# A safety margin in a planner's clock: operands of TensorE and freed buffers of the second layer count as ready later

## The chip, the core and the metric

The kernel runs on one core of a Trainium2 chip. The metric is device time in microseconds of one execution; lower is better. TensorE is PE in the profile, its weight loads are PEld, VectorE is DVE, ScalarE is ACT, GpSimd is POOL, SyncE is SP. SP only issues DMAs here; POOL issues some and computes a little.

## The reference, cut to what matters

Two layers over 512 rows of width 1024, all in float32. Layer 0 is a retention layer, layer 1 is a forgetting attention with 16 heads of width 64:

```python
q, k, v, g, f = jnp.split(h @ w_in, [FOX_W, 2 * FOX_W, 3 * FOX_W, 4 * FOX_W], axis=-1)
q = _rms_norm(q.reshape(b, s, 16, 64), q_gain) * (64 ** -0.5);  k = _rms_norm(k..., k_gain)
cum = jnp.cumsum(log_sigmoid(f + b_f), axis=1)
for qs in range(0, s, 128):              # 128 queries at a time
    logits = q[qs:qe] @ k[:qe].T + cum[qs:qe, None] - cum[None, :qe]
    p = softmax(where(causal, logits, -inf))
    outs.append(p @ v[:qe])
return (o * silu(g)) @ w_out
x = x + gate * y                         # after each layer; a last RMSNorm closes
```

## The kernel before, in words

**Arithmetic.** Each float32 operand of a matmul is split into a rounded upper half and the rest, and a product is three matmuls (`mm3`: upper x upper, upper x rest, rest x upper). For a weight tile `raw` (512 KB, loaded by SP) ACT casts the upper half `wh` and DVE subtracts to get the rest `wl`. One matmul of 128x128 by 128x512 is the unit of PE's work.

**Layer 1 in stages.** First come the projections of queries and keys (names `p<-wh,sf`, `p<-wh,big`: `big` holds the layer's normalised input, `sf` sums of it) and the forget gates (`wf`, `z`, `tri`, `cum_dram`). Then for each head: PE transposes the normalised rows `qn` and DVE and ACT write them as stacked halves `st` (`stacks`); PE multiplies queries by keys (`r<-st,st`, `scores`, four blocks a head); DVE adds the mask and the cumulated gates and writes `lg`; ACT takes the exponential; DVE the reciprocal; POOL multiplies `lg` by it; PE transposes `lg` (`r<-ident,lg`, `turn`); ACT and DVE write the halves `ph`; PE multiplies them by `v` (`r<-ph,v`, `values`, eight matmuls a head); DVE and ACT write `oT`. Between these steps PE works at projections (of the second half of q, k, v and of the gate g), which wait for nothing in the heads. At the end the output projection (`a<-wh,goh`) and the last norm follow.

**Buffers.** PE's results go to eight PSUM banks: kinds `p` (projections, at most six) and `r` (everything of the heads, at most four). A bank is used again when its last reader is done. All other tiles share pools of fixed slots in the same way.

**What sets the order.** The program is not written in the order in which it runs. Each call makes a `Task` with a priority; `Sched.order` then runs the whole program through a model of the engines, with a clock of its own: a task may start on its engine when all it depends on is done, `LAT` = 0.2 us after the end of a producer on another engine, and when the buffers it writes first are free. Each engine takes the task with the lowest priority number of those that may start. The order in which the model starts the tasks is the order in which they are emitted, engine by engine, all from one line (L472 in the profile's rows). On the chip each engine works through its list in that order, and waits on semaphores where the chip is later than the model. So a number in the model changes no instruction, only what stands ahead of what on each engine.

The two places of the model that the change touches are these:

```python
b.users -= 1
if b.users == 0 and b.kind is not None:
    free[self.kinds[b.kind][0]].append(b.slot)
    used[b.kind] -= 1
...
lat = self.LAT if t.eng != s.eng else 0.0 if t.eng == "PE" else 0.13
s.ready = max(s.ready, t.done + lat)
```

Of the kernel before, what the change touches and what calls it, by code (L numbers as in the profile page):

```python
# [26 lines left out]
PE = mybir.EngineType.PE  # L27
# [33 lines left out]
LATER = 4.0  # L61

GATE1 = "q k v g0"

LOOK = 30.0

# [130 lines left out]
class Sched:  # L197
# [117 lines left out]
    def order(self):  # L315

        import heapq
        tasks = self.tasks
        free = {k: list(range(n)) for k, (n, _) in self.phys.items()}
        used = {k: 0 for k in self.kinds}  # L320
        turn = {k: 0 for k in self.kinds}
        avail = {e: [] for e in self.ENG.values()}
        busy = {e: True for e in avail}
        ev, count, out, table = [(START, 0, -i, e, None) for i, e in enumerate(busy)], 0, [], None
        hw = dma = reach = 0.0
        soft, soft_wait, soon = [], [], []
        ticks = {-1: 0}
        left = sum(t.eng == "PE" for t in tasks)
        for t in tasks:
            t.wait, t.ready = len(t.deps), 0.0  # L330
            if not t.wait:
                heapq.heappush(avail[t.eng], (t.prio, t.seq, t))

        def fits(t):
            if t.eng == "SP" and t.prio > reach:
                return False
            need = {}
            t.new = [b for b in t.bufs if b.slot is None and b.kind is not None]
            for b in t.new:
                ph, cap = self.kinds[b.kind]  # L340
                need[ph] = need.get(ph, 0) + 1
                if turn[b.kind] != b.seq or used[b.kind] >= cap or len(free[ph]) < need[ph]:
                    return False
            return True

        now = 0.0
        while True:
            moved = True
            while moved:
                moved = False  # L350
                for e in avail:
                    if busy[e]:
                        continue
                    held, got = [], None
                    while avail[e]:
                        x = heapq.heappop(avail[e])
                        if fits(x[2]):
                            got = x[2]
                            break
                        held.append(x)  # L360
                    for x in held:
                        heapq.heappush(avail[e], x)
                    if got is not None and e == "DVE" and now < LOOK and any(
                            x.prio < got.prio - 1.0 and x.ready < now + 0.2 and fits(x) for x in soon):
                        heapq.heappush(avail[e], (got.prio, got.seq, got))
                        continue
                    if got is None and e == "PE" and now > 1.5 and self.idle is not None and self.idle.buf.slot is not None:

                        got = self.filler()
                    if got is None:  # L370
                        continue
                    moved = True
                    if self.idle is not None and e == "PE" and not got.filler and self.idle.buf in got.bufs:
                        self.idle = None
                    for b in got.new:
                        ph = self.kinds[b.kind][0]
                        b.slot = free[ph].pop(0)
                        used[b.kind] += 1
                        turn[b.kind] += 1
                    out.append(got)  # L380
                    got.start = now
                    if e == "PE":
                        tick = int(now / TICK)
                        if ticks.get(tick - 1, 0) < TICK_COLS and got.cols > 192:
                            got.cost *= 2.0
                        tick = int((now + got.cost) / TICK)
                        ticks[tick] = ticks.get(tick, 0) + got.cols
                    if e == "PE":
                        left -= not got.filler or got is self.first
                        reach = max(reach, got.prio) if left else now + 1e9  # L390
                    busy[e] = True
                    count += 1
                    end = now + got.cost
                    if got.table not in (None, table):
                        end += 1.3
                        table = got.table
                    heapq.heappush(ev, (end, 0, count, e, None))
                    if got.bytes:
                        if e == "POOL":
                            soft.append(got)  # L400
                            a = end + 0.6
                        else:
                            hw = max(hw, now + 0.05) + 0.45
                            a = hw + 0.6
                        heapq.heappush(ev, (a, 3, count, None, got))
                    else:
                        got.done = end
                        heapq.heappush(ev, (end, 1, count, None, got))
            if not ev:
                break  # L410
            now = ev[0][0]
            while ev and ev[0][0] <= now:
                _, what, _, e, t = heapq.heappop(ev)
                if what == 0:
                    busy[e] = False
                elif what == 3 and t.eng == "POOL" and t is not soft[0]:

                    soft_wait.append(t)
                elif what == 3:
                    dma = max(now, dma) + t.bytes / 360e3  # L420
                    t.done = dma + 0.5
                    if t.eng == "POOL":
                        t.done = now + t.bytes / 360e3 + 1.4
                    count += 1
                    heapq.heappush(ev, (t.done, 1, count, None, t))
                elif what == 1:
                    if t.bytes and t.eng == "POOL":
                        soft.pop(0)
                        if soft and soft[0] in soft_wait:
                            count += 1  # L430
                            soft_wait.remove(soft[0])
                            heapq.heappush(ev, (now, 3, count, None, soft[0]))
                    for b in t.bufs:
                        b.users -= 1
                        if b.users == 0 and b.kind is not None:
                            free[self.kinds[b.kind][0]].append(b.slot)
                            used[b.kind] -= 1
                    for s in t.next:
                        lat = self.LAT if t.eng != s.eng else 0.0 if t.eng == "PE" else 0.13
                        s.ready = max(s.ready, t.done + lat)  # L440
                        s.wait -= 1
                        if not s.wait:
                            count += 1
                            heapq.heappush(ev, (s.ready, 2, count, None, s))
                            if s.eng == "DVE":
                                soon.append(s)
                else:
                    if t in soon:
                        soon.remove(t)
                    heapq.heappush(avail[t.eng], (t.prio, t.seq, t))  # L450
        if ev or any(avail.values()):
            todo = {e: [(t.emit[1], [(b.kind, b.seq) for b in t.new]) for _, _, t in sorted(avail[e])[:4]]
                    for e in avail}
            raise RuntimeError(f"stuck at {now:.1f} of {len(tasks) - len(out)} tasks: {todo}, {used}, {turn}")
        self.end = now
        return out
# [98 lines left out]
def trunk(tc, x, c, positions, mod_w, mod_b, norm_g, ret_w_in, ret_w_out, fox_w_in, fox_b_f,  # L555
# [6 lines left out]
    with ExitStack() as es:  # L562
# [255 lines left out]
        def add(key, its):  # L818
            where[key] = len(items)
            items.extend(its)  # L820
# [93 lines left out]
        def gate_after(key):  # L914
            for _ in range(GATE1.split().count(key)):
                add(("e", len(items)), extra.pop(0))
# [969 lines left out]
```

## Time and profile before

| what | value |
|---|---|
| median of 3 runs | 714.42 us (714.22 to 714.66) |
| the profiled execution: its time, its span | 714.6 us, 712.6 us |
| PE, PEld busy | 700.3 us (98%), 576.7 us (81%) |
| DVE, ACT, POOL busy | 617.5 us (87%), 420.2 us (59%), 128.0 us (18%) |
| granted clock of PE, mean | 0.998 |
| HBM read, written | 113.35 MB, 4.25 MB |

The span is the time from the first to the last instruction; 2.0 us of the execution lie around it. Times in the rows below are counted from the span's start. A row of the timeline gives start, duration, engine, line, operation, output<-inputs, array size, shape, and in brackets how long the engine sat idle before it and which engine's instruction ended that; "x7" is seven instructions in a row. A matmul's shown duration is longer than the distance to the next one's start, because matmuls are pipelined: two rows of PE overlap. Layer 1 fills the span from about 420 us.

### The profile page before, as it was taken

The numbers are of one execution on the slowest core, as the hardware profiler recorded it, in microseconds if no ns is written. First come the engines' busy times: TensorE is split into PE (matmuls) and PEld (weight loads), VectorE is DVE, ScalarE is ACT, GpSimd is POOL, SyncE is SP. The second block draws the span as 40 slices with busy tenths as digits, with TensorE's granted clock in tenths as the row PEclk, the third lists the DMA queues.
The fourth block names the chain that finished last, engine by engine and source line by source line (L and its number), as shares of the span: only waits on it lengthen the run. The fifth ranks groups of instructions, "written<-read, shape, count | busy, mean of one in ns | idle before, by whom it ended". The sixth has DMA issues, their size and how long they took to land.

```text
span 712.6 us, 10207 instructions
## 1 busy us (share of the span) xinstructions
PE 700.3 (98%) x3383; PEld 576.7 (81%) x3383; DVE 617.5 (87%) x1268; ACT 420.2 (59%) x779; POOL 128.0 (18%) x175
## 2 busy tenths in 40 slices
PE   8999999999999999999999999999999999999995
PEld 6888888888888888888888887787877888888884
DVE  4799999888978996998998899699898998789925
ACT  5558564654365435865534565674777677779613
POOL 1001101100010001001000102014463564442011
PEclk9999999999999999999999999999999999999999
DMA  8992964647666766717669315668776696757002
GB/s 285 349 327 86 183 211 82 140 164 265 128 152 206 236 121 158 269 60 147 186 203 296 147 41 118 126 210 196 202 165 169 178 214 152 184 132 232 36 14 104
DMA packets 80724, 122.47 MB, mean 172 GB/s; under 512 B 7080, under 2 KB 39968, under 8 KB 80672
## 3 DMA queue, kind: packets, MB, share of 16 engines
q1 hardware_dynamic: 66176, 98.71, 43.2%
q0 software_dynamic: 14496, 23.10, 19.0%
q8 instruction: 27, 0.44, 0.3%
q14 instruction: 25, 0.20, 0.1%
HBM read 113.35 MB, written 4.25 MB: 165 GB/s over the span
## 4 chain that ended last, share of the span: by engine, by line
PE 82%; DVE 12%; ACT 3%; issue 2%; DMA 0%; POOL 0%; DVEq 0%; ACTq 0%; POOLq 0%
PE p L472 48%; PE r L472 17%; PE a L472 11%; PE s L472 6%; DVE wl L472 2%; DVE t L472 2%; DVE st L472 1%; DVE qn L472 1%; DVE xn L472 1%; DVE lg L472 1%; DVE ph L472 1%; ACT st L472 1%; ACT lg L472 1%; ACT wh L472 1%; DVE x L472 1%
## 5 line engine op out<-in xcount | busy, mean ns | idle before, releaser
L472 DVE TENSOR_TENSOR wl<-raw,wh 128x1024 fp32r<-128x1024 f32 x132 | 160.5, 1219 | 27.8 <-PE p L472 16.2
L472 ACT CAST wh<-raw 128x1024 fp32r<-128x1024 f32 x132 | 137.3, 1051 | 76.7 <-PE p L472 37.7
L472 PE MATMUL p<-wh,big 128*128 128x512 f32 x304 | 102.8, 400 | 0.0
L472 PE MATMUL p<-wh,sf 128*128 128x512 f32 x320 | 101.6, 392 | 0.0
L472 PEld LDWEIGHTS p<-wh,sf 128*128 128x128 f32 x320 | 60.0, 188 | 12.8
L472 PEld LDWEIGHTS p<-wh,big 128*128 128x128 f32 x304 | 56.8, 189 | 10.7
L472 POOL DMA_DIRECT2D raw<-in_ret_w_in x16 | 19.4, 1212 | 255.9 <-DMA raw<-in_mod_w 78.2
L472 PE MATMUL p<-wh,act 128*128 128x512 f32 x192 | 62.7, 393 | 0.0
L472 PE MATMUL p<-wl,sf 128*128 128x512 f32 x160 | 62.7, 392 | 0.0
L472 PE MATMUL p<-wl,big 128*128 128x512 f32 x152 | 60.7, 400 | 0.0
L472 POOL TENSOR_SCALAR lg<-lg,t 128x512 f32<-128x512 f32 (+1 forms) x64 | 46.9, 838 | 67.5 <-DVE t L472 64.5
L472 DVE SCALAR_TENSOR_TENSOR macc<-raw,csilu,macc 128x512 f32<-128x512 f32 x76 | 57.1, 753 | 0.8
L472 PE MATMUL p<-act,wh 128*128 128x512 f32 x160 | 53.4, 393 | 0.0
L472 ACT ACTIVATE lg<-lg,t 128x512 f32<-128x512 f32 (+1 forms) x64 | 35.7, 559 | 13.8 <-DVE t L472 13.5
L472 PE MATMUL p<-big,wh 128*128 128x512 f32 x128 | 43.6, 403 | 0.0
L472 PE MATMUL r<-act,sh 128*128 128x512 f32 x120 | 42.7, 391 | 0.2 <-DVE sh L472 0.2
L472 PEld LDWEIGHTS p<-wh,act 128*128 128x128 f32 x192 | 36.0, 188 | 7.3
L472 PE MATMUL p<-wh,go 128*128 128x512 f32 x112 | 39.2, 402 | 0.0
L472 PE MATMUL p<-wl,act 128*128 128x512 f32 x96 | 37.8, 394 | 0.0
L472 PEld LDWEIGHTS p<-wl,sf 128*128 128x128 f32 x160 | 30.0, 188 | 6.1
L472 PE MATMUL r<-st,st 128*128 128x512 f32 (+3 forms) x128 | 34.1, 337 | 0.5 <-DVE st L472 0.3
L472 PEld LDWEIGHTS p<-act,wh 128*128 128x128 f32 x160 | 29.8, 188 | 5.6
(213 smaller groups left out, 1592.9 us busy)
## 6 DMA issues: line engine op xcount, KB each, us to landing
raw<-in_ret_w_in SPq DMA_DIRECT2D x48, 512.0 KB, 5.3
raw<-in_mod_w SPq DMA_DIRECT2D x64, 256.0 KB, 6.0
raw<-in_fox_w_in SPq DMA_DIRECT2D x32, 512.0 KB, 4.6
raw<-in_ret_w_in POOLq DMA_DIRECT2D x16, 512.0 KB, 6.4
raw<-in_mod_w SPq DMA_DIRECT2D x16, 512.0 KB, 4.4
raw<-in_ret_w_out SPq DMA_DIRECT2D x16, 512.0 KB, 4.9
ck<-cum_dram SPq DMA_DIRECT2D x16, 448.0 KB, 4.8
x<-in_x SPq DMA_DIRECT2D x16, 256.0 KB, 5.9
```

The source lines that it names most:

```text
L472: getattr(eng, op)(*[real(v) for v in args], **{k: real(v) for k, v in kw.items()})
```

## The change

Three numbers are added to the model, and used only where its clock is past 420: an operand that another engine makes for PE counts as ready 0.8 us later than before, and a freed buffer (a PSUM bank or a slot of any pool) counts as free 0.5 us later.

```diff
+MARGIN, FREE, MARGIN_FROM = 0.8, 0.5, 420.0
...
+                elif what == 4:
+                    free[self.kinds[t.kind][0]].append(t.slot)
+                    used[t.kind] -= 1
...
                         if b.users == 0 and b.kind is not None:
-                            free[self.kinds[b.kind][0]].append(b.slot)
-                            used[b.kind] -= 1
+                            count += 1
+                            heapq.heappush(ev, (now + (FREE if now > MARGIN_FROM else 0.0), 4, count, None, b))
                     for s in t.next:
                         lat = self.LAT if t.eng != s.eng else 0.0 if t.eng == "PE" else 0.13
+                        if s.eng == "PE" and t.eng != "PE" and now > MARGIN_FROM:
+                            lat += MARGIN
```

No instruction is added, removed or resized. The lists of all engines stay as they were up to the forget gates of layer 1; behind that point most rows of PE, DVE and ACT have moved by a few places. (Line 472 of the kernel before is line 480 after, and buffer numbers count in the order of emission, so the same tile may carry another number.)

First place, PE, the first scores of the first head (about 493 to 495 us in the trace before). `qn` rows are the transposes whose result DVE and ACT turn into `st`; the first row with `st` is the one that needs it. Before, from the last transposes on:

```order
L472 MATMUL r_4852<-ident,qn_4742 128x128
L472 MATMUL r_4861<-ident,qn_4742 128x128
L472 MATMUL p_4751<-wh_4706,big_3988 128x512
L472 MATMUL p_4751<-wl_4797,big_3988 128x512
L472 MATMUL p_4751<-wh_4706,big_4000 128x512
L472 MATMUL p_4751<-wh_4706,big_3988 128x512
L472 MATMUL p_4751<-wl_4797,big_3988 128x512
L472 MATMUL p_4751<-wh_4706,big_4000 128x512
L472 MATMUL p_4766<-wh_4706,big_3988 128x512
L472 MATMUL p_4766<-wl_4797,big_3988 128x512
L472 MATMUL r_4890<-st_4753,st_4875 128x512
L472 MATMUL r_4890<-st_4760,st_4875 128x512
```

After, from the third matmul behind the last transposes on:

```order
L480 MATMUL p_4766<-wh_4710,big_3988 128x512
L480 MATMUL p_4766<-wl_4806,big_3988 128x512
L480 MATMUL p_4766<-wh_4710,big_4000 128x512
L480 MATMUL p_4766<-wh_4710,big_3988 128x512
L480 MATMUL p_4766<-wl_4806,big_3988 128x512
L480 MATMUL p_4766<-wh_4710,big_4000 128x512
L480 MATMUL p_4783<-wh_4710,big_3988 128x512
L480 MATMUL p_4783<-wl_4806,big_3988 128x512
L480 MATMUL p_4783<-wh_4710,big_4000 128x512
L480 MATMUL p_4783<-wh_4710,big_3988 128x512
L480 MATMUL r_4903<-st_4754,st_4879 128x512
L480 MATMUL r_4903<-st_4760,st_4879 128x512
```

Before, eight projection matmuls stand between the last transposes and the first scores; now it is twelve.

Second place, PE, the first value matmul of a late head (about 632 to 635 us in the trace before). The `lg` row is the last of the four transposes whose result ACT and DVE turn into `ph`. Before:

```order
L472 MATMUL r_6653<-ident,lg_6472 128x128
L472 MATMUL p_6621<-big_3979,wl_6210 128x512
L472 MATMUL p_6537<-big_3988,wh_6350 128x512
L472 MATMUL p_6537<-big_4000,wh_6350 128x512
L472 MATMUL p_6537<-big_3988,wl_6365 128x512
L472 MATMUL p_6537<-big_3988,wh_6350 128x512
L472 MATMUL p_6537<-big_4000,wh_6350 128x512
L472 MATMUL r_6673<-ph_6666,v_5916 128x512
L472 MATMUL r_6675<-st_6535,st_6613 128x512
L472 MATMUL r_6680<-ident,lg_6566 128x128
L472 MATMUL p_6537<-big_3988,wl_6365 128x512
L472 MATMUL p_6537<-big_3988,wh_6350 128x512
```

After:

```order
L480 MATMUL p_6505<-big_3988,wl_6325 128x512
L480 MATMUL p_6505<-big_3988,wh_6307 128x512
L480 MATMUL p_6505<-big_4000,wh_6307 128x512
L480 MATMUL p_6505<-big_3988,wl_6325 128x512
L480 MATMUL p_6505<-big_3988,wh_6307 128x512
L480 MATMUL p_6505<-big_4000,wh_6307 128x512
L480 MATMUL r_6688<-ph_6669,v_5905 128x512
L480 MATMUL r_6690<-st_6545,st_6613 128x512
L480 MATMUL r_6690<-st_6560,st_6613 128x512
L480 MATMUL r_6688<-ph_6675,v_5905 128x512
L480 MATMUL r_6688<-ph_6609,v_5927 128x384
L480 MATMUL r_6688<-ph_6624,v_5927 128x384
```

The piece of after begins two matmuls behind the last `lg` transpose: eight matmuls now stand ahead of the first value matmul, before it was six. The second value matmul, which needs DVE's half of `ph`, stood seven rows behind the first; now it stands three rows behind.

Third place, PE, the end of the attention: the last value matmuls of the last head and what is left behind them up to the output projection. Before, with nine more projection matmuls below the piece that is shown:

```order
L472 MATMUL r_6940<-ph_6901,v_6065 128x128
L472 MATMUL r_6940<-ph_6916,v_6065 128x128
L472 MATMUL p_6777<-big_3988,wl_6618 128x512
L472 MATMUL p_6777<-big_3988,wh_6598 128x512
L472 MATMUL p_6777<-big_4000,wh_6598 128x512
L472 MATMUL p_6777<-big_3988,wl_6618 128x512
L472 MATMUL p_6777<-big_3988,wh_6598 128x512
L472 MATMUL p_6777<-big_4000,wh_6598 128x512
L472 MATMUL p_6777<-big_3988,wl_6618 128x512
L472 MATMUL p_6871<-big_3988,wh_6598 128x512
L472 MATMUL p_6871<-big_4000,wh_6598 128x512
L472 MATMUL p_6871<-big_3988,wl_6618 128x512
```

After, up to the first row of the output projection:

```order
L480 MATMUL r_6959<-ph_6906,v_6094 128x128
L480 MATMUL r_6959<-ph_6913,v_6094 128x128
L480 MATMUL p_6839<-big_3988,wl_6573 128x512
L480 MATMUL p_6839<-big_3988,wh_6552 128x512
L480 MATMUL p_6839<-big_4000,wh_6552 128x512
L480 MATMUL p_6839<-big_3988,wl_6573 128x512
L480 MATMUL p_6839<-big_3988,wh_6552 128x512
L480 MATMUL p_6839<-big_4000,wh_6552 128x512
L480 MATMUL p_6839<-big_3988,wl_6573 128x512
L480 MATMUL a_7003<-wh_6678,goh_6946 128x512
```

Seven projection matmuls are left behind the last head where there were nineteen.

## The prediction

> **What bounds the kernel now.** I read the page's busy line and its chain first, then PE by stretches, then PE's waits, then the timeline at these waits.
>
> ```profile
> PE 700.3 (98%) x3383; PEld 576.7 (81%) x3383; DVE 617.5 (87%) x1268; ACT 420.2 (59%) x779; POOL 128.0 (18%) x175
> PE 82%; DVE 12%; ACT 3%; issue 2%; DMA 0%; POOL 0%; DVEq 0%; ACTq 0%; POOLq 0%
> ```
>
> PE is busy nearly always, yet 12% of the chain runs through DVE. So there are places where PE stood because DVE was late. The stretches tell where (columns: PE, PEld, DVE, ACT, POOL busy with counts, granted clock, DMA share, GB/s):
>
> ```profile
> 240.00:280.00 40.00, 40.00 (x188) 33.45 (x187) 35.09 (x74) 15.03 (x26) 4.83 (x4) 1.00 0.63 156
> 420.00:460.00 40.00, 39.73 (x176) 30.00 (x175) 32.53 (x60) 26.45 (x42) 4.89 (x4) 1.00 0.50 106
> 460.00:500.00 40.00, 39.19 (x179) 31.14 (x178) 38.22 (x69) 23.14 (x31) 9.61 (x14) 1.00 0.70 185
> 500.00:540.00 40.00, 39.58 (x213) 32.58 (x213) 34.44 (x94) 29.00 (x74) 21.22 (x31) 1.00 0.77 191
> 540.00:580.00 40.00, 39.64 (x212) 32.48 (x211) 37.29 (x90) 28.77 (x68) 20.33 (x30) 1.00 0.76 190
> 580.00:620.00 40.00, 39.46 (x219) 33.14 (x218) 34.37 (x85) 30.84 (x74) 20.77 (x32) 1.00 0.66 162
> 620.00:660.00 40.00, 39.55 (x221) 33.14 (x220) 35.54 (x86) 33.28 (x78) 13.80 (x22) 1.00 0.64 188
> ```
>
> A stretch of layer 0 has no idle PE at all; layer 1's six stretches have 237.15 of 240 busy, 2.85 us idle. The clock is full throughout, so no part of this is a slower clock. PE's waits between 420 and 660 are short and all on the heads' steps, none on a weight:
>
> ```profile
> PE r L472 <- DVE st L472: 0.6, 2, 0.4
> PE r L472 <- ACT ph L472: 0.5, 2, 0.3
> PE r L472 <- DVE qn L472: 0.4, 1, 0.4
> PE r L472 <- DVE oT L472: 0.3, 1, 0.3
> PE r L472 <- DVE t L472: 0.3, 1, 0.3
> PE r L472 <- ACT z L472: 0.3, 1, 0.3
> ```
>
> The idle time understates the loss, because a row's duration covers part of the gap behind it. The loss is the distance of two starts, less the usual distance. The usual one is in the chain: 192 matmuls in 42.89 us and 19 in 4.39 are 0.22 and 0.23 us each.
>
> ```profile
> 657.34 4.39 PE p L472 x19
> 661.73 42.89 PE a L472 x192
> ```
>
> Against that, these pairs of neighbours on PE, in order of time:
>
> ```profile
> 455.77 0.39 PE L472 MATMUL p<-wl,sf 128*128 128x512 f32 x1
> 456.44 0.40 PE L472 MATMUL r<-tri,z 128*16 128x512 f32 x1 [0.27 <-ACT z L472]
> ...
> 489.62 0.39 PE L472 MATMUL p<-wh,big 128*128 128x512 f32 x1
> 490.38 1.15 PE L472 MATMUL r<-ident,qn 128*128 128x128 f32 x8 [0.38 <-DVE qn L472]
> ...
> 494.13 0.40 PE L472 MATMUL p<-wl,big 128*128 128x512 f32 x1
> 494.81 1.48 PE L472 MATMUL r<-st,st 128*128 128x512 f32 x4 [0.28 <-DVE st L472]
> ...
> 551.73 0.39 PE L472 MATMUL p<-wl,big 128*128 128x512 f32 x1
> 552.45 0.52 PE L472 MATMUL r<-ident,lg 128*128 128x128 f32 x3 [0.33 <-DVE t L472]
> ...
> 633.59 0.62 PE L472 MATMUL p<-big,wh 128*128 128x512 f32 x2
> 634.53 0.50 PE L472 MATMUL r<-ph,v 128*128 128x512 f32 x1 [0.32 <-ACT ph L472]
> ...
> 650.33 0.62 PE L472 MATMUL p<-big,wh 128*128 128x512 f32 x2
> 651.09 1.27 PE L472 MATMUL r<-ph,v 128*128 128x512 f32 x7
> ```
>
> From 489.62 to 490.38 is 0.76, less 0.23 is 0.53 us lost, where the row shows 0.38 idle. The last pair shows no idle time and loses 0.76 less two steps, 0.3. Taken so for every neighbouring pair, each against the usual distance of its shape, 37 places between these first and last rows lose more than 0.04 us each, 7.3 us together. That is all a better order can bring in this stage, since projections stand ready to fill it. Fifteen places of 0.12 us or more hold 5.25 us; the other 22 hold 2.0, most of them the next matmul or two behind a wait.
>
> The 15 are of two kinds. At seven (2.7 us) the operand itself came last, as `st` at 494.81 and `ph` at 634.53. At eight (2.55 us) the operand had long been there and the PSUM bank came last. So at 552.45: POOL makes the `lg` that is transposed, yet the wait is put down to DVE, whose last read of the bank ends at 551.88 + 0.42 = 552.30.
>
> ```profile
> 551.88 0.42 DVE L472 TENSOR_TENSOR ph<-r,ph 128x256 fp32r<-128x256 f32 x1
> ```
>
> **A rule on headroom.** By the Trainium skill ("Perfetto Trace Analysis", section "Identifying the Most-Contended Engine"), matmul busy time is no good measure of how near TensorE is to its limit, and the busy share of the weight loads is better. The rows agree as far as the first half goes: 2.85 us idle stands for 7.3 lost. Measured by its second half, the six stretches hold 192.48 us of weight loads; at the 33.45 per 40 us of the unbroken stretch these would fill 230.2 us, so 9.8 us would be lost; regaining the share of it that the sum below regains of 7.3 (4.75) would give 714.4 - 6.4 = 708.0. I keep 7.3, because the mix of shapes differs.
>
> **The change part by part.** It adds and removes no instruction. What it does is to put more projection matmuls between a cause on PE and the PE instruction that needs its effect.
>
> *Operands, 0.8 us.* Of the seven waits the largest is 0.53 us, less than the margin. The pieces of the order agree at two of them: four matmuls more ahead of the first scores (4 x 0.23 = 0.9 against 0.45 lost there) and two more ahead of the value matmul (0.46 against 0.94 - 0.46 = 0.48). The others, counted in the order in the same way: over 0.7 us more at 456.44, 490.38 and 615, nothing more at 651.09, and 0.7 us less at 644. What grows holds 2.3 us; I take 2.2 gained of 2.7. Bounds: 0, if DVE and ACT run as much later as PE asks later; 2.7, if all goes.
>
> *Freed buffers, 0.5 us.* The eight bank waits are 0.13 to 0.52 us, the largest as long as the margin itself. DVE is late by a different amount at each place, as these waits show, and some places will meet more than 0.5, so I leave a quarter: 1.95 of 2.55 gained. Bounds 0 and 2.55. A slot of SBUF freed later makes some loads count later; that is hidden by the lead of the weights, below.
>
> *Followers.* The 22 small ones go with the waits that they follow: 2.0 x 0.75 = 1.5. Bounds 0 and 2.0.
>
> *New waits.* Other pairs move closer: the second value matmul stood seven rows behind the first and now stands three. If DVE's half of `ph` was just in time, this costs up to 4 x 0.23 = 0.9 us in a head; if it was early, nothing. Counted over the heads, five places lose distance and most of these by under 0.5 us. I take 0.9 us for all, bounds 0 and 3.
>
> *The end.* The chain shows 19 projection matmuls (4.39 us) between the last head and the output projection, and 7 are left now, 1.6 us. This cover is spent between the heads. It costs nothing while the last head's `ph` comes less than 1.6 us late, and the longest wait of that kind is 0.5. Behind it PE runs 42.89 us without a wait, and the rest hangs on that as before.
>
> Sum: 2.2 + 1.95 + 1.5 - 0.9 = 4.75, say 4.8 us. The profiled execution took 714.6 us (span 712.6 and 2.0 around it), so 709.8 for it; it lies 0.2 above the median 714.42, so 709.6 for the median.
>
> **Rivals.**
>
> *All of it goes:* the margins exceed every wait but one, so 714.4 - 7.3 = 707.1. Against it: places where the distance shrank.
>
> *DVE is the next bound.* In 460:500 it is busy 38.22 of 40, in 540:580 37.29. If those two stretches keep their waits (0.53 + 0.45 + 0.31 and 0.49 + 0.22 + 0.13 = 2.1 us) and the followers, 0.5, the gain is 2.2 and the time 712.2. For it: an order of PE cannot make DVE finish earlier. Against it: 1.8 us of DVE's 40 are free even there.
>
> *POOL's multiplications come late.*
>
> ```profile
> L472 POOL TENSOR_SCALAR lg<-lg,t x64: 361/688/1895, 501.9 to 651.7; 128x512 f32<-128x512 f32 x16, 128x384 f32<-128x384 f32 x16, 128x256 f32<-128x256 f32 x16, 128x128 f32<-128x128 f32 x16
> ```
>
> One takes 0.69 us in the median and up to 1.9. In the new order other DVE work lies beside them; if one in four heads loses the 1.2 us between, of which 0.7 is covered by the margin, that is 4 x 0.5 = 2 us less gain, 711.6. No PE wait above is on POOL. The Trainium skill ("SBUF — State Buffer", section "SBUF: two separate sides") says that VectorE and GpSimd lock a shared port pair for a whole instruction, which would make such spreads.
>
> *The waits only change places:* 714.4. For it: the order moved nearly all rows at once. Against it: every move is away from a late operand.
>
> *Slower: weights of the projections land late.* Freed slots count later, so loads may be asked for later. One landed so late that ACT sat for 4.86 us; and where the lead is smallest, DVE's `wl` ends at 458.78 + 1.22 = 460.0 and PE needs it at 461.55.
>
> ```profile
> 489.88 1.05 ACT L472 CAST wh<-raw 128x1024 fp32r<-128x1024 f32 x1 [4.86 <-DMA raw<-in_fox_w_in]
> 458.78 3.80 DVE L472 TENSOR_TENSOR wl<-raw,wh 128x1024 fp32r<-128x1024 f32 x3
> 461.55 0.39 PE L472 MATMUL p<-wl,sf 128*128 128x512 f32 x1
> ```
>
> A load that is 4.86 us late costs 4.86 - 1.5 = 3.3 us there; two of them outweigh 4.8 and give 714.4 + 6.6 - 4.8 = 716.2. Against it: no PE wait is on a weight.
>
> **How the numbers follow.** Chances: the sum as above (gain 3.3 to 6.3) 0.54; all of it 0.12; DVE the bound 0.16; POOL late 0.05; waits only moved 0.08; late weights 0.05. The time is that of the first, 709.6, its own range 708.1 to 711.1. The range 707.3 to 712.9 leaves out the last two and the outermost part of "all". Faster or slower counts from 0.2% on, 1.4 us, about what a measurement of this kernel can tell: faster 0.87, same 0.08, slower 0.05.
>
> **What would show it.** In the profile after: idle PE in 420 to 660 falls from 2.85 us to under 1.2, the waits on `st`, `qn`, `oT` and `z` vanish from the list, and DVE's share of the chain falls from 12% to under 6%. The output projection starts 4 to 5.5 us earlier than at 661.7 and still takes 42.9. Remaining waits should be on `ph` and on banks. I am wrong if PE waits on `wl` or `wh`, if POOL's `lg` appears as what PE waits for, or if DVE's idle time between 460 and 500 is gone with PE's waits still there.

## The result, and the profile after

| | before | after |
|---|---|---|
| median (lowest to highest) | 714.32 us (713.92 to 714.66) | 710.34 us (709.66 to 710.90) |
| the profiled execution, its span | 714.6, 712.6 us | 710.33, 708.4 us |

The ratio is 0.9946, with a 95% interval of 0.9934 to 0.9958: 4.0 us less. 709.6 was forecast, with a range of 707.3 to 712.9. All views below are of the kernel after unless another is named. First the page's busy line and the shares of the chain:

```profile
PE 695.8 (98%) x3383; PEld 576.0 (81%) x3383; DVE 616.8 (87%) x1268; ACT 419.6 (59%) x779; POOL 127.4 (18%) x175
PE 90%; DVE 6%; ACT 1%; issue 1%; DMA 1%; POOL 0%; DVEq 0%; POOLq 0%; ACTq 0%
```

The counts are the same, and no engine has less work to do; DVE's share of the chain has halved from 12%. Then layer 1 by stretches (PE, PEld, DVE, ACT, POOL busy with counts, granted clock, DMA share, GB/s):

```profile
420.00:460.00 40.00, 40.00 (x178) 30.76 (x178) 34.48 (x63) 27.53 (x43) 4.89 (x4) 1.00 0.50 106
460.00:500.00 40.00, 39.81 (x186) 32.15 (x185) 36.36 (x70) 23.07 (x34) 9.63 (x14) 1.00 0.70 187
500.00:540.00 40.00, 39.97 (x217) 33.37 (x216) 35.81 (x94) 30.54 (x77) 21.47 (x33) 1.00 0.75 190
540.00:580.00 40.00, 39.11 (x209) 32.03 (x208) 37.53 (x92) 27.16 (x64) 19.81 (x28) 1.00 0.74 184
580.00:620.00 40.00, 39.95 (x227) 33.97 (x226) 33.43 (x85) 31.44 (x78) 20.23 (x33) 1.00 0.71 174
620.00:660.00 40.00, 40.00 (x222) 34.31 (x220) 37.12 (x85) 33.79 (x76) 14.05 (x22) 1.00 0.64 189
```

PE's waits from 420 to 660 (us in total, times, longest):

```profile
PE r L480 <- DVE ph L480: 0.6, 2, 0.3
PE r L480 <- DVE st L480: 0.5, 2, 0.3
```

PE's idle time fell from 2.85 us to 1.16, and three quarters of it now lies in one stretch, 540 to 580, where DVE is busiest (37.53 of 40). The waits on `qn`, `oT`, `z` and ACT's `ph` have left the list. At the three places of before that the rows of the prediction showed (490.38, 494.81, 634.53), PE now goes straight on; the pairs in order of time are:

```profile
488.80 0.39 PE L480 MATMUL p<-wh,big 128*128 128x512 f32 x1
489.06 0.66 PE L480 MATMUL r<-ident,qn 128*128 128x128 f32 x4
...
493.66 0.61 PE L480 MATMUL p<-wh,big 128*128 128x512 f32 x2
494.11 1.01 PE L480 MATMUL r<-st,st 128*128 128x512 f32 x4
...
631.57 0.62 PE L480 MATMUL p<-big,wh 128*128 128x512 f32 x2
632.03 0.40 PE L480 MATMUL r<-ph,v 128*128 128x512 f32 x1
```

From 488.80 to 489.06 is 0.26 (0.76 before), from 493.66 to 494.11 is 0.45 for two matmuls, and 631.57 to 632.03 is 0.46. The first is only just so: the `qn` that it needs was done at 489.00, 0.06 us before; at the other two the operand had been done for 0.5 us. What is left is of another kind and at other places:

```profile
563.79 0.48 PE L480 MATMUL p<-wl,big 128*128 128x512 f32 x1
564.52 0.72 PE L480 MATMUL r<-st,st 128*128 128x512 f32 x2 [0.25 <-DVE ph L480]
...
570.46 0.62 PE L480 MATMUL p<-wh,big 128*128 128x512 f32 x2
571.38 0.44 PE L480 MATMUL r<-st,st 128*128 128x128 f32 x2 [0.29 <-DVE st L480]
572.12 0.63 PE L480 MATMUL r<-ident,lg 128*128 128x128 f32 x4 [0.31 <-DVE ph L480]
```

Scores do not read `ph`, and transposes of `lg` do not either: at 564.52 and 572.12 what came last was the bank that DVE's `ph` had been reading. At 571.38 the name misleads in another way. Scores do read `st`, but by the kernel's list the last of the `st` that these scores read was written in the first of the following two rows of DVE's timeline, and the second row makes other `st` from the bank that the scores need:

```profile
546.66 1.51 DVE L480 SCALAR_TENSOR_TENSOR st<-r,gain,st 64x512 fp32r<-64x512 f32 x2
...
569.81 1.51 DVE L480 SCALAR_TENSOR_TENSOR st<-r,gain,st 64x512 fp32r<-64x512 f32 x2 [0.54 <-ACT st L480]
```

The operand was done at 548.17, the bank was free at 571.32. The other wait on `st` in the list above, at 496.02, is of the same kind: its operand had been done for 2.4 us. Taken by the distance of two starts as in the prediction, with each wait followed by its instruction, the 37 places with 7.29 us are 22 with 3.96 now. The chain's last rows of PE:

```profile
650.51 2.30 PE p L480 x10
657.06 42.89 PE a L480 x192
```

The last instruction of ACT in the timeline of before:

```profile
708.03 0.72 ACT L472 ACTIVATE x<-x,t 128x512 f32<-128x512 f32 x1 [1.56 <-DVE t L472]
```

And in that of after:

```profile
703.36 0.72 ACT L480 ACTIVATE x<-x,t 128x512 f32<-128x512 f32 x1 [1.56 <-DVE t L480]
```

The output projection starts 661.73 - 657.06 = 4.67 us earlier, takes the same 42.89, and ACT's last instruction is 4.67 earlier too. Behind that the span goes on for 712.6 - 708.03 = 4.57 us before and 708.4 - 703.36 = 5.04 after, so 0.47 is lost at the last stores, and 4.2 us of the span is left. Of the 4.67, 0.40 was there before the first row that moved, in work that both kernels do in the same order, as the timeline's row of the transposes of `xn` shows. Before:

```profile
413.36 1.09 PE L472 MATMUL r<-ident,xn 128*128 128x128 f32 x8
```

After:

```profile
412.96 1.09 PE L480 MATMUL r<-ident,xn 128*128 128x128 f32 x8
```

### The profile page after: what moved, and what is told of

The parts are those of the page before. It is cut to its first block, busy times and chain, and to the rows that moved or that the text cites. A ratio compares the mean times of both kernels' runs of the same rounds, so it can differ in the third digit from the quotient of the medians.

```text
span 708.4 us, 10215 instructions
## 1 busy us (share of the span) xinstructions
PE 695.8 (98%) x3383; PEld 576.0 (81%) x3383; DVE 616.8 (87%) x1268; ACT 419.6 (59%) x779; POOL 127.4 (18%) x175
## 4 chain that ended last, share of the span: by engine, by line
PE 90%; DVE 6%; ACT 1%; issue 1%; DMA 1%; POOL 0%; DVEq 0%; POOLq 0%; ACTq 0%
PE p L480 56%; PE r L480 18%; PE a L480 11%; PE s L480 5%; DVE st L480 1%; DVE xn L480 1%; DMA vrow<-in_mod_b 1%; DVE t L480 1%; ACT st L480 1%; DVE x L480 1%; DVE ph L480 0%; DVE macc L480 0%; DVE wl L480 0%; DVE lg L480 0%; DVE big L480 0%
## 5 line engine op out<-in xcount | busy, mean ns | idle before, releaser
L480 PE MATMUL p<-wh,big 128*128 128x512 f32 x304 | 99.8, 397 | 0.0
L480 POOL TENSOR_SCALAR lg<-lg,t 128x512 f32<-128x512 f32 (+1 forms) x64 | 41.0, 671 | 72.1 <-DVE t L480 66.9
L480 DVE TENSOR_TENSOR ph<-r,ph 128x128 fp32r<-128x128 f32 (+1 forms) x64 | 30.6, 482 | 3.8 <-ACT ph L480 3.2
```

The lines of the kernel that those rows point to most:

```text
L480: getattr(eng, op)(*[real(v) for v in args], **{k: real(v) for k, v in kw.items()})
```

## The experiments

Each wait of 0.12 us or more was followed to the instruction that waits, in every kernel. "Old" are waits of instructions that are among the 15 of before; "new" are the others; "small" are places of 0.04 to 0.12. A wait counts as operand or bank by what was done last in the trace: the tile that the instruction reads, or the last read of the bank that it writes, both known from the kernel's list. "Left" is the number of projection matmuls behind the last head. All in us, the losses from the profiled execution of 420 to 660.

| kernel (operands, buffers) | left | old | new | of old and new: operand / bank | small | median | ratio, 95% interval |
|---|---|---|---|---|---|---|---|
| before (0, 0) | 19 | 5.25 | 0 | 2.69 / 2.56 | 2.04 | 714.4 | 1 |
| after (0.8, 0.5) | 7 | 0.98 | 2.00 | 0.21 / 2.77 | 0.97 | 710.34 | 0.9946 [0.9934, 0.9958] |
| operands only (0.8, 0) | 5 | 0.98 | 3.57 | 0.43 / 4.13 | 1.43 | 712.43 | 0.9976 [0.9966, 0.9986] |
| buffers only (0, 0.5) | 28 | 2.25 | 2.34 | 2.88 / 1.71 | 1.88 | 713.64 | 0.9991 [0.9983, 1.0000] |
| buffers twice (0.8, 1.0) | 0 | 0.29 | 4.42 | 2.65 / 2.07 | 1.42 | 714.16 | 0.9992 [0.9980, 1.0003] |
| negative (-0.2, 0) | 24 | 4.79 | 2.72 | 5.21 / 2.30 | 3.17 | 718.00 | 1.0053 [1.0040, 1.0066] |
| (0.8, 1.0 to 580, then 0.5) | 11 | 0.29 | 2.23 | 0.43 / 2.09 | 1.23 | 709.61 | 0.9933 [0.9920, 0.9947] |
| cost of `st` (0, 0) | 17 | 1.70 | 3.57 | 2.32 / 2.94 | 1.97 | 714.03 | 0.9997 [0.9989, 1.0006] |
| (0.4, 0.5) | 16 | 1.16 | 1.32 | 0.93 / 1.56 | 1.18 | 709.74 | 0.9936 [0.9924, 0.9949] |
| twice, with the gap filled | 0 | 0.30 | 2.21 | 0.45 / 2.05 | 1.37 | 712.42 | 0.9971 [0.9961, 0.9982] |
| (0.75, 0.55) | 12 | 0.37 | 1.94 | 0 / 2.31 | 1.23 | 710.03 | 0.9938 [0.9926, 0.9950] |
| (0.8, 0.5) to 540 only | 26 | 2.03 | 2.92 | 1.39 / 3.56 | 1.37 | 712.25 | 0.9967 [0.9955, 0.9979] |
| (0.3, 1.0 to 580, then 0.5) | 12 | 0.87 | 1.72 | 2.01 / 0.58 | 1.32 | 710.34 | 0.9947 [0.9935, 0.9960] |
| (0.4, 0.5), cost of `st` | 11 | 0.26 | 2.09 | 0.22 / 2.13 | 1.26 | 710.22 | 0.9946 [0.9934, 0.9959] |

### The two margins apart

```diff
-MARGIN, FREE, MARGIN_FROM = 0.8, 0.5, 420.0
+MARGIN, FREE, MARGIN_FROM = 0.8, 0.0, 420.0
```

> MARGIN 0.8, FREE 0: the operands' margin alone. Theory A (the 0.8 us on operands did the gain, the 0.5 us on buffers nothing): 710.3 us, 709.5 to 711.2, as the whole change; operand waits of 0.12 us or more on PE between 420 and 660 sum to under 0.5 us, bank waits to 2 to 3.3. Rival B (both margins share the gain, as the prediction's sum had it, 2.2 and 1.95): 712.0 to 712.8. Rival C (any other order of these instructions would have scattered around the same time): anywhere from 710 to 716, without a pattern in the waits.

712.43 us. The old operand waits are all gone, and of the old bank waits only 0.98 of 2.56 is left, though no bank counted later; but 3.14 us of bank waits are new. The largest, 1.05 us, is at the scores of 495.43, which lost 0.11 before (their own `st` was done at 493.02); and a wait on POOL's `lg` appears, the only one of any kernel here. Both in this kernel's timeline of PE:

```profile
495.43 0.50 PE L480 MATMUL r<-st,st 128*128 128x256 f32 x2 [0.88 <-DVE st L480]
...
652.84 0.66 PE L480 MATMUL r<-ident,lg 128*128 128x128 f32 x4 [0.27 <-POOL lg L480]
```

```diff
-MARGIN, FREE, MARGIN_FROM = 0.8, 0.5, 420.0
+MARGIN, FREE, MARGIN_FROM = 0.0, 0.5, 420.0
```

> MARGIN 0, FREE 0.5: the buffers' margin alone. Theory A: 713.6 to 715.0, within 0.1% of before; operand waits stay at 2 to 3.5 us and bank waits at 2 to 3. Rival B: 712.0 to 712.8, bank waits under 1 us. Rival C: no pattern.

713.64 us: the operand waits stay (2.88), the bank waits fall to 1.71. So the operands' margin alone brings 2.0 us and the buffers' 0.75 (its interval reaches to 1.0000), together 2.7; both at once bring 4.0. That the operands do it all is wrong, and so is that the two add: B's time came with the operands alone and not with the buffers alone. The second margin is worth 712.43 - 710.34 = 2.1 us once the first is there: it takes away a part of the bank waits that the first one makes, 4.13 to 2.77, and 0.46 of the small places.

### More, and less than nothing

```diff
-MARGIN, FREE, MARGIN_FROM = 0.8, 0.5, 420.0
+MARGIN, FREE, MARGIN_FROM = 0.8, 1.0, 420.0
```

> MARGIN 0.8, FREE 1.0: buffers count as free 1.0 us later. No projection matmul is left behind the last head in the order (7 with the change, 19 before). Theory A with a longer bank margin: bank waits fall from 2.8 to under 1.5 us, since the longest was 0.5 behind a margin of 0.5; but with the cover spent the last heads' chain shows, 1 to 3 us on waits for ph and lg between 640 and 660: 709.5 to 712.5. If bank waits do not answer to the margin at all: they stay at 2.5 us or more, and the time is 711 to 714.

Of 12 runs 9 took 714.0 to 714.8 us and 3 took 711.3 to 712.3, the median 714.16. Between the heads the bank waits are 2.07 us instead of 2.77, but the end cover is spent, and PE stands in front of the last head's value matmul, as this kernel's timeline shows:

```profile
655.45 0.60 PE L480 MATMUL r<-ident,lg 128*128 128x128 f32 x4
657.70 0.50 PE L480 MATMUL r<-ph,v 128*128 128x512 f32 x1 [1.65 <-ACT ph L480]
658.22 0.50 PE L480 MATMUL a<-wh,goh 128*128 128x512 f32 x1
658.55 0.40 PE L480 MATMUL a<-wl,goh 128*128 128x512 f32 x1
658.79 0.39 PE L480 MATMUL a<-wh,goh 128*128 128x512 f32 x1
659.02 1.87 PE L480 MATMUL r<-ph,v 128*128 128x512 f32 x7
660.69 1.16 PE L480 MATMUL a<-wh,goh 128*128 128x512 f32 x2
661.65 0.63 PE L480 MATMUL a<-wl,goh 128*128 128x512 f32 x1
662.08 0.63 PE L480 MATMUL a<-wh,goh 128*128 128x512 f32 x1
662.50 0.43 PE L480 MATMUL a<-wl,goh 128*128 128x512 f32 x1
662.77 0.62 PE L480 MATMUL a<-wh,goh 128*128 128x512 f32 x2
```

Three stretches of the same kernel (columns as above, the clock is the third number from the end):

```profile
655.00:660.00 5.00, 3.33 (x15) 2.42 (x14) 5.00 (x11) 4.95 (x11) 0.00 (x0) 0.92 0.52 200
660.00:665.00 5.00, 5.00 (x20) 4.20 (x19) 4.94 (x9) 4.95 (x10) 0.00 (x0) 0.74 0.00 2
665.00:670.00 5.00, 5.00 (x23) 4.14 (x23) 5.00 (x8) 2.66 (x6) 0.00 (x0) 1.00 0.01 3
```

The wait costs 1.65 us, and then the granted clock drops: 0.08 x 5 + 0.26 x 5 = 1.7 us more. The rows show the same. At 658.55 and 658.79 the next matmul still starts 0.24 and 0.23 us later; at 661.65 and 662.08 it starts 0.43 and 0.42 later; and from 662.77 on two matmuls take 0.62 again. Neither expectation has this run: bank waits of 2.07 lie between the two, and 714.16 is far above the first range of time and just above the second, because the one long wait costs the clock as well.

```diff
-MARGIN, FREE, MARGIN_FROM = 0.8, 0.5, 420.0
+MARGIN, FREE, MARGIN_FROM = -0.2, 0.0, 420.0
```

> MARGIN -0.2, FREE 0: operands of other engines count for PE 0.2 us earlier than before the change, at their producer's end. Theory A: more and longer operand waits, 3.5 to 6 us instead of 2.7, so 715.3 to 718. Rival C (scatter of orders): as likely faster as slower, 711 to 717, operand waits unchanged.

718.00 us, 3.6 more than with no margin, the top of theory A's range. Three of this kernel's seven waits of PE:

```profile
PE r L480 <- ACT ph L480: 1.8, 4, 0.6
PE r L480 <- DVE qn L480: 0.6, 1, 0.6
...
PE r L480 <- ACT z L480: 0.5, 1, 0.5
```

These are the waits of before, longer and more of them: operands came 0.2 us earlier in the model and the operand waits grew from 2.69 to 5.21. So the sign of the margin decides, not that the order was shaken.

### Where the clock went

```diff
-MARGIN, FREE, MARGIN_FROM = 0.8, 0.5, 420.0
+MARGIN, FREE, MARGIN_FROM = 0.8, 1.0, 420.0
...
+        spare, turned = pt_(), [t for t in s.tasks if t.emit[1] == "transpose"][-1]
+        with s.after(turned):
+            for _ in range(8):
+                T.matmul(spare, ones_r, ones_r.unsqueeze(1).to_broadcast([P, 4, P]), start=True, stop=True)
```

> As the run with freed buffers at 1.0 us, with eight matmuls of ones into an unused PSUM bank placed in the wait of 1.65 us that stands before the last head's value matmul (their result is read by nothing; they are work added, 8 x 0.23 = 1.8 us, in a gap of 1.65 us). Theory 'the gap made the clock fall': that run's granted clock was 0.92 and 0.74 in the 10 us behind the gap, and its output projection, which started 1.3 us later than the changed kernel's, ended 4.1 us later. With the gap filled the clock is 1.00 from 655 to 670 and the projection takes its usual time: 711.5 to 713 us, without single runs near 714. Rival 'the clock fell for another reason': the clock still falls behind the last head, 714.2 us or up to 1.8 later.

712.42 us, with all 8 runs between 711.91 and 712.96. The same place in this kernel's timeline:

```profile
655.52 2.10 PE L480 MATMUL p<-ones_r 128*128 128x512 f32 x8
657.62 0.50 PE L480 MATMUL r<-ph,v 128*128 128x512 f32 x1
```

And its stretches:

```profile
655.00:660.00 5.00, 5.00 (x28) 4.04 (x27) 4.83 (x10) 4.95 (x11) 0.00 (x0) 1.00 0.33 127
660.00:665.00 5.00, 5.00 (x24) 4.12 (x24) 4.94 (x9) 4.95 (x10) 0.00 (x0) 1.00 0.02 5
```

With useless work in the gap the clock stays at 1.00 and the kernel is 1.7 us faster. That the gap made the clock fall is shown for this place; transposes stand right ahead of the gap, or of the filler, in both kernels. The three quick runs of the kernel without the filler have no trace. Their mean granted clocks are 0.996, 0.998 and 0.996, those of the other nine 0.994 (six) and 0.996 (three): this fits with a clock that fell in most of the nine and not in the three, but does not settle it, and the two groups are some 2.5 us apart, more than the 1.7 us.

### Sizes of the margins

```diff
-MARGIN, FREE, MARGIN_FROM = 0.8, 0.5, 420.0
+MARGIN, FREE, MARGIN_FROM = 0.8, 1.0, 420.0
...
-                            heapq.heappush(ev, (now + (FREE if now > MARGIN_FROM else 0.0), 4, count, None, b))
+                            heapq.heappush(ev, (now + (0.0 if now < MARGIN_FROM else FREE if now < 580.0 else 0.5), 4, count, None, b))
```

> As the changed kernel, but freed buffers count 1.0 us later up to model time 580 and 0.5 us from there on. 11 projection matmuls stay behind the last head (7 with the change, none with 1.0 us throughout). Theory 'a bank's wait is a distance that the order can buy' (the changed kernel still loses 2.77 us at ten bank waits, of which seven lie before 600): the bank waits fall to under 1.6 us in all, no long wait stands before the last head's value matmul, the output projection starts at 655.8 or before, 708.5 to 709.7 us. Rival 'bank waits do not answer to more margin' (they come from DVE being late by an amount that the order itself sets): bank waits stay at 2.5 to 3 us and the time at 710 to 711 us.

709.61 us (709.33 to 710.61; the profiled run is the slowest of its five). The long wait in front of the last head is gone and the time is the one forecast, but the bank waits, 2.09 us, are neither under 1.6 nor at 2.5 to 3, and its interval overlaps the changed kernel's. Neither theory is borne out.

```diff
-MARGIN, FREE, MARGIN_FROM = 0.8, 0.5, 420.0
+MARGIN, FREE, MARGIN_FROM = 0.4, 0.5, 420.0
```

> Operands count 0.4 us later instead of 0.8, freed buffers 0.5 us as in the change. With operands at 0 the seven operand waits hold 2.9 us (713.64), with 0.8 they hold 0.2 (710.34). If the margin works as a distance that each late operand either fits into or not: of waits of 0.13 to 0.53 us most fit, operand waits 0.5 to 1.2 us, 711 to 712 us. If any margin that reorders the heads does it: 710.3. If the threshold lies above 0.4: 713 to 714 us.

709.74 us. The operand waits are 0.93, inside what was expected for a margin that some waits fit into, but the time lies 1.3 us under what that theory gave and nearest to the 710.3 of "any margin": the bank waits fell with the margin, from 2.77 to 1.56, so that operand and bank together hold 2.5 us instead of 3.0.

```diff
-MARGIN, FREE, MARGIN_FROM = 0.8, 0.5, 420.0
+MARGIN, FREE, MARGIN_FROM = 0.3, 1.0, 420.0
```

> Operands 0.3 us, freed buffers 1.0 us up to model time 580 and 0.5 us from there; 12 projection matmuls stay behind the last head. With 0.4 and 0.5 the losses were 0.93 us at operands and 1.56 at banks, with 0.8 and 0.5 0.21 and 2.77, with 0.8 and 1.0 until 580 0.43 and 2.09. Theory 'the filler between the heads is limited, and what one margin takes the other lacks': operand waits of 0.8 to 1.2 us, bank waits of 1 to 1.6 us, 709 to 710.3 us. Rival 'each margin works on its own kind alone': operand waits 0.9 us and bank waits under 1, 708 to 709 us; or, if 0.3 is too little for the operands (their waits are 0.13 to 0.53 us), operand waits over 1.6 us and 711 us or more.

(The rule for 1.0 up to 580 is that of the first run of this section.) 710.34 us: operand waits of 2.01, bank waits of 0.58. The operand waits are the third case's (over 1.6), the bank waits the second's (under 1), the time the top of the first's. What holds is the exchange: with 0.8 and 0.5 nearly all of the loss is at banks, with 0.3 and 1.0 nearly all of it at operands, and the sum is 3.0 and 2.6.

```diff
-MARGIN, FREE, MARGIN_FROM = 0.8, 0.5, 420.0
+MARGIN, FREE, MARGIN_FROM = 0.75, 0.55, 420.0
```

> Margins of 0.75 and 0.55 us instead of 0.8 and 0.5; 12 projection matmuls stay behind the last head. The planner gives another order with nearly the same margins, so the time shows how far a mere rearrangement moves it. Theory 'the margin decides, not the particular order': within 0.7 us of the changed kernel's 710.34, 709.6 to 711.0. Rival 'the order found with 0.8 and 0.5 was a lucky one': 712 us or more, with operand waits back.

710.03 us, as the theory said, with no operand wait of 0.12 us or more and nine bank waits, seven of them new. So the changed kernel's gain does not hang on its particular order.

### A better figure instead of a margin

```diff
-MARGIN, FREE, MARGIN_FROM = 0.8, 0.5, 420.0
+MARGIN, FREE, MARGIN_FROM = 0.0, 0.0, 420.0
...
+        late = 0.1 if any(v.buf.kind == "st" for v in outs) else 0.0
-        return 0.069 + 0.061 * ptr + n / (1920.0 if fast else 960.0)
+        return late + 0.069 + 0.061 * ptr + n / (1920.0 if fast else 960.0)
```

> Both margins zero; only the planner's cost of the DVE instructions that write the state tile st is 0.1 us higher (the trace's step of these 32 is 0.096 us longer than the planner's figure, 3.1 us of DVE in all; its other DVE and ACT figures agree within 0.01 us). Theory 'the waits come from one wrong figure in the planner': operand and bank waits fall from 5.2 us to under 3.5, 712 to 713 us. Rival 'the waits come from the spread of single instructions and of signals, which no mean holds': losses stay within 1 us of before's 8.7, 713.9 to 715 us.

714.03 us, ratio 0.9997 [0.9989, 1.0006]: no change that can be told. The old waits fell from 5.25 to 1.70 and 3.57 new ones came; with the small places 7.24 us are lost, and 7.29 before. (The 8.7 in the expectation is not from the count used here.) The rival is right: one wrong figure does not make the waits. This is what "the waits only change places" looks like: another order, with the traced figure for `st` in it and no slack.

```diff
-MARGIN, FREE, MARGIN_FROM = 0.8, 0.5, 420.0
+MARGIN, FREE, MARGIN_FROM = 0.4, 0.5, 420.0
```

> Operands 0.4 us, freed buffers 0.5 us, and the planner's cost of the DVE instructions that write st 0.1 us higher; 11 projection matmuls stay behind the last head. The 0.4 and 0.5 kernel took 709.74 us, and of its waits of 0.12 us or more six, 1.4 us, are on st itself or on a bank that an st instruction frees. The higher cost alone gave 714.03. Theory 'the true cost and the margin add': 708.2 to 709.3 us. Rival 'the margin covers that figure already': 709.4 to 710.5 us.

(The cost of `st` is raised here too.) 710.22 us: the figure adds nothing to the margin, as the rival said.

### Place by place

```diff
-                            heapq.heappush(ev, (now + (FREE if now > MARGIN_FROM else 0.0), 4, count, None, b))
+                            heapq.heappush(ev, (now + (FREE if MARGIN_FROM < now < 540.0 else 0.0), 4, count, None, b))
...
-                        if s.eng == "PE" and t.eng != "PE" and now > MARGIN_FROM:
+                        if s.eng == "PE" and t.eng != "PE" and MARGIN_FROM < now < 540.0:
```

> Margins 0.8 and 0.5 us between model times 420 and 540 only, none after; 26 projection matmuls stay behind the last head. By places, before loses 3.5 us in 420 to 540 and 3.8 us in 540 to 660, the changed kernel 1.35 and 2.6. Theory 'the gain is made place by place, where a wait stood': the first half's 2.2 us are gained and the second half's waits stay, 711.8 to 712.8 us, with waits on st and qn gone before 540 and waits on ph or banks of 3 us and more after it. Rival 'the gain comes from one shift of the whole order, or from the end' : 710.3 or 714.4 us.

712.25 us: 2.2 us gained, the time that the theory gave. PE's waits of this kernel from 420 to 540:

```profile
PE r L480 <- DVE st L480: 0.2, 1, 0.2
```

From 540 to 660:

```profile
PE r L480 <- DVE st L480: 0.8, 2, 0.5
PE r L480 <- ACT ph L480: 0.7, 2, 0.4
PE r L480 <- DVE t L480: 0.2, 1, 0.2
```

Up to 540 the places hold 1.25 us, as in the changed kernel (1.35): where the margins acted, the waits went. From there they hold 5.1 (the theory had 3 or more), and before held 3.8: the second half's waits did not just stay but grew by 1.3, and 26 projection matmuls left over at the end did not help. By the places only 0.9 us would be gained in all; the profiled execution's span is 712.6 - 711.0 = 1.6 shorter and the median 2.2. The theory is borne out for the first half; that its time came true for the whole is in part luck.

## Why the prediction was right, and where it was not

The mechanism was right: with slack in the planner PE's old waits went, and in each of the seven other orders with both margins over the whole layer they fell as well, from 5.25 us to 1.16 or less (the long wait at the end of the run with 1.0 us is a new one). Two terms of the sum were mis-sized, both towards too much gain: new waits by 1.1 us and followers by 0.4. The median still came within 0.74 us of the forecast, because 0.93 us was gained outside the sum; that part is luck. By instructions:

| term | forecast | measured |
|---|---|---|
| operands, 7 waits | +2.2 | 2.69 - 0.21 = +2.48 |
| freed buffers, 8 waits | +1.95 | 2.56 - 0.77 = +1.79 |
| followers | +1.5 | 2.04 - 0.97 = +1.07 |
| new waits | -0.9 | -2.00 |
| sum | +4.75 | +3.34 |
| in no place over 0.04 us | | +0.93 |
| before the first moved row | | +0.40 |
| at the last stores | | -0.47 |
| span | | +4.2 |

**Operands.** Six of the seven are gone; the one that is left, at 615.18, is on ACT's `ph` with 0.21 (0.35 before). It was among those whose distance was said to have grown enough. The two where the distance was said to stay or to shrink (651.09 and 644.20) are gone: DVE's half of `ph` is done there 0.36 and 0.59 us before PE comes to it. So matmuls counted between cause and effect on PE did not tell in every case which wait would go; DVE's order has changed too.

**Freed buffers.** Five of the eight are gone. The quarter held back was about right (0.77 of 2.56 is left); but that is not the margin for buffers alone, since the operands' margin by itself removed 1.6 of these 2.56.

**New waits.** This is the step that failed. The prediction looked for them where value matmuls had come closer to `ph`, at 0.9 us. No such wait is there in the trace after: in the second place of the change, where the second value matmul had come closest, it starts at 632.72, 0.14 us after its `ph` is done. The seven new ones are all at banks, 2.0 us, on DVE's last read. (One of them, 0.29 us at the scores of 548.77, is not quite new: these scores lost some 0.2 us before, at 550.17, and were not counted among the 15.) The runs show where they come from: with the operands' margin alone the new bank waits are 3.1, and the buffers' margin brings them to 2.0. In six orders with both margins over the whole layer and some matmuls left at the end, old and new waits together hold 2.3 to 3.0 us and the times lie between 709.6 and 710.3, whether operands or banks hold the loss. The bound of 0 to 3 us had this; the value taken was too near to the low end.

**Followers.** They went with their waits, and the new waits brought some of their own.

**The end.** As forecast: cover of 19 matmuls came down to 7 at no cost, and the projection still takes 42.89. The condition stated for it, the last head's `ph` within 1.6 us, is borne out from the other side: with no matmul left, PE stands for 1.65 us there.

**What was to be seen.** Idle PE under 1.2 us (1.16), the projection 4 to 5.5 us earlier (4.67), no wait on weights or `lg`: so it came. DVE's share of the chain was to be under 6% and is shown as 6%. Waits on `st` were to vanish from the list, and two, 0.5 us, are in it; both are waits for banks, of the kind that was expected to remain.

**The terms that the sum did not have.** 0.93 us was gained in no place that the rows single out; why, stays open. The 0.40 lies in work that both kernels do in the same order. What the 0.47 at the last stores comes from, no run tells.

**Rivals.** *All of it goes* (707.1): no order's median came under 709.6. *DVE is the next bound* (712.2): half right in its place, not in its size. 540 to 580 holds 0.89 of the 1.16 us that PE idles, and 1.9 of the 3.0 us in waits, but 460 to 500 kept only 0.5 of its 1.3 us. Whether DVE's speed sets the remaining 2.3 to 3.0 us was not tried. *POOL's `lg` late* (711.6): the median did not rise but fell, from 688 to 577 ns, and no wait on it is there:

```profile
L480 POOL TENSOR_SCALAR lg<-lg,t x64: 361/577/1882, 500.7 to 649.2; 128x512 f32<-128x512 f32 x16, 128x384 f32<-128x384 f32 x16, 128x256 f32<-128x256 f32 x16, 128x128 f32<-128x128 f32 x16
```

With the operands' margin alone it did appear, once, with 0.27 idle. What makes the spread of these multiplications, no run shows. *The waits only change places* (714.4) is what the higher cost of `st` did, without a margin. *Late weights* (716.2): no wait of PE on a weight.

**The rule on headroom.** The six stretches now hold 196.59 us of weight loads, 192.48 before; at 33.45 per 40 us that is 235.1 of 240, so 4.9 us would be lost now and 9.8 before. By the places it is 3.96 and 7.29. The output projection came 4.67 us earlier, 4.27 without the 0.40 from before this stage: between the 3.3 of the places and the 4.9 of the weight loads. The Trainium skill's advice to judge by the loads ("Perfetto Trace Analysis", section "Identifying the Most-Contended Engine") did well here where idle time, 1.7 us less, did badly. Its forecast of 708.0 was too low because it took the forecast's share, 0.65, as regained; by the loads it was half.

## What to carry to other kernels

A planner that knows the mean durations still puts a consumer just behind its operand; a few tenths of a microsecond of slack in its model, where other work is ready, was worth more here than the one better figure that was tried. Slack for operands alone turned operand waits into waits for buffers, so both needed it, and then the exact sizes mattered little as long as some filler was left at the end. Count what the slack spends: the filler it moves forward is missing at the end of the stage, and there a wait costs its own length and perhaps the clock behind it.

## What the runs showed of the hardware

A gap of 1.65 us in PE's work was followed by a granted clock of 0.92 and 0.74 in two windows of 5 us (1.7 us of clock lost). The fall came only after PE was at work again: matmuls at 658.55 and 658.79 still took 0.24 and 0.23 us each, those at 661.65 and 662.08 took 0.43 and 0.42. Filling that gap with eight useless matmuls kept the clock at 1.00 and took 1.7 us off the time. The Trainium skill ("TensorE: Matmul & The Clock Gate", section "HAM oscillation — how this bites in real kernels") gives as the rule that there be no idle gaps over about 3.4 us; here half of that was enough in the profiled run. Gaps of 0.88 us (operands only, at 495.43), 0.83 (buffers only, at 494.56) and 0.70 (1.0 us to 580, at 514.12) showed no such drop: the clock is 1.00 in the windows of 5 us that hold them and in those behind.

In the views a matmul that waits for a bank is put down to the tile that the bank's last reader wrote (`ph` for the scores at 564.52 and for the transposes at 572.12). A wait named with a tile that the instruction does not read is a wait for a buffer. The reverse does not hold: the scores at 571.38 read `st`, are put down to `st`, and waited for a bank all the same.
